# Hybrid decoder trunk: attention weights as differences of a scan, stick queries and keys projected as feature rows, narrower dilated scores

## Chip, core and metric

One core of a Trainium2 chip runs the whole program. TensorE multiplies and transposes, VectorE (DVE), ScalarE (ACT) and GpSimd (POOL) do elementwise work, and the queue of SyncE (SP) issues the transfers. The metric is the device time of one execution in microseconds.

## What is computed

Two layers, each `x = x + concat(A, B) @ w_out`, on x of 2048 x 1024 in fp32. One input projection of the normalised x gives queries, keys, values and gates for two mixers.

- A, stick-breaking attention, 4 heads of 64: `z = q k / 8`; `log_surv = log_sigmoid(z) - z` for earlier keys; `a = exp(log_sigmoid(z) + sum of log_surv over later keys)`; `o = a v`. So a weight is sigmoid(z) times the product of sigmoid(-z) over all keys between it and the query.
- B, dilated window attention, 12 heads of 64: three patterns (window 128 step 1, 512 step 4, 2048 step 16), each a softmax over at most 129 keys per query, mixed by their denominators. Queries and keys are normalised and partly rotated.

Each mixer's output is multiplied by a SiLU gate.

## The kernel before

Almost all products run in a rounded fp32 format (F32R); where precision asks for it, an operand is split into a high and a low part and three products are summed. The stages of a layer follow each other: normalise and transpose x (`prep` of `Project`), projection (`run`), stick attention (`_stick`), dilated attention (`_dilated`), output (`_output`). A planner orders the instructions of each engine, except that those marked `pin` keep their order in the program on TensorE.

**Projection.** `mm3` multiplies 128 tokens (stationary) by 512 columns of weights (streaming), in 8 steps of k with three products each. Two token blocks form a group; four PSUM banks (`pm`) hold two groups. First come the values of A (`narrow("sb", ...)`), then the list `wide`: queries and keys of A together (`"sb"`), three blocks of queries and keys of B (`"qk"`, evacuated by `qk_out`: squares, sum, power on GpSimd, multiply, rotation, split, transposes), a block of values of B. `tail` has the rest; gates go the other way round (weights stationary, 512 tokens streaming). Queries, keys and values of A are written to `sb_scr`, one row per token. During the last tail block, `inject` starts work of `_stick`.

**Stick.** `prep(pr, jq)` for a pair of heads and a quarter of the tokens loads rows of queries and keys, splits them into high and low parts, transposes 16 blocks (L504), copies them (L507) to feature rows, and lets two transfers swap the halves of the keys into `sh` (L509, L510). The first pair's four quarters are injected into the projection; the second pair's run between the first pair's units.
A unit is 128 queries against up to 512 keys, from late keys to early ones; a layer has 80 units of two heads. `front` makes the scores (L541, L542, and L544 for the mask), two sigmoids (L549, L550), a running product from the end (L551) and on GpSimd the weight (L557):

```
g = sigmoid(-z/8);  b = sigmoid(z/8)
r[k] = r[k+1] * g[k]          (scan, carried from unit to unit)
b = b * r[k+1]
```

`mid` transposes the weights (L570) and copies them (L572), the first head on ScalarE, the second on VectorE. `back` multiplies by the values (L584). `front` runs `LEAD` = 2 units ahead of `mid`; `back` is called for `BATCH` = 2 units at once. Slots: 6 for `r`, 6 for `g`, 6 for `b`, 6 for the copied weights.

**Dilated.** Six pairs of heads, three patterns, 16 blocks of 128 queries: 48 steps a pair. `front` makes four score products (two heads, two halves of the split, L732), adds the mask and takes the minimum on VectorE (L734), and exponentiates on ScalarE (L738). `mid` transposes (L753) and copies (L755), alternately on ScalarE and VectorE; `back` multiplies by values (L767) for four blocks. All score products stream 256 columns; pattern 0, and the first blocks of the other patterns, use only 128 of them. In later pairs, `stats_a` and `stats_b` work out the weights of the mixture of the pair before; `weigh` broadcasts them by a product (L837) and multiplies (L838), in steps 15 to 30, after `mid` and `back`. `mid` reads one of four `pe` slots.

The functions that the diff touches:

Of the kernel before, what the change touches and what calls it, by code (L numbers as in the profile page):

```python
# [115 lines left out]
def kernel(ctx, tc, x, norm_g, w_in, q_g, k_g, w_out, rope, masks, sel, out,  # L116
# [24 lines left out]
    for layer in range(depth):  # L141
        last = layer == depth - 1
        L = f"l{layer}"
        sb_scr = dram.tile([3, S, 256], F32, name=f"sb_{L}")
# [12 lines left out]
        sb = _stick(tc, mem, sb_scr, g_scr, mix, ident, ident_r)  # L157
# [5 lines left out]
        proj.run(sb_scr, v_scr, qk_scr, g_scr, inject)  # L163
# [25 lines left out]
class Project:  # L189
# [96 lines left out]
    def run(self, sb_scr, v_scr, qk_scr, g_scr, inject):  # L286
# [25 lines left out]

        def v_out(i, n, src, c):
# [10 lines left out]
        def sb_out(i, n, src, c):  # L324
            for j in range(n):
                nc.sync.dma_start(out=sb_scr[i + j].rearrange("(a c) d -> a c d", c=NT)[:, c],
                                  in_=src[:, 256 * j:256 * j + 256])
# [48 lines left out]
        wide = [("sb", 0, [(0, QA, 512)])]  # L376
# [28 lines left out]
        for bi, (kind, idx, parts) in enumerate(wide):  # L405
            nxt = wide[bi + 1][2] if bi + 1 < len(wide) else None
            for g in range(NT // 2):
# [5 lines left out]
                for k in range(NK) if edge else (None,):  # L413
                    for j in range(2):
                        for kk in range(NK) if k is None else (k,):
                            mm3(pss[j], 2 * g + j, kk, *self.wide(kk))
# [8 lines left out]
                if kind == "qk":  # L425
                    qk_out(idx, pss, 2 * g)
                    continue
                for j, ps in enumerate(pss):
                    st = stg.get([128, 512])
                    (nc.scalar.copy if j else nc.vector.tensor_copy)(st, ps)  # L430
                    (sb_out if kind == "sb" else v_out)(idx, 2, st, 2 * g + j)

        for bi, (kind, idx, parts) in enumerate(tail):
# [9 lines left out]
            for gi, (ct, tq) in enumerate(order):  # L443
# [4 lines left out]
                w = slice(128 * ct, 128 * ct + 128)  # L448
                ps = pm.get([128, 512])
                for k in range(NK):  # L450
                    nc.tensor.matmul(ps, wh[:, k, w], hT(tq, 0, k), start=k == 0, stop=False)  # L451
                    nc.tensor.matmul(ps, wh[:, k, w], hT(tq, 1, k), start=False, stop=False)  # L452
                    nc.tensor.matmul(ps, wl[:, k, w], hT(tq, 0, k), start=False, stop=k == NK - 1)  # L453
# [6 lines left out]
def _stick(tc, mem, sb_scr, g_scr, mix, ident, ident_r):  # L460
# [10 lines left out]
    raw_r = mem.ring("H0", "H1")  # L471
    q2_r = mem.ring("F12", "F13")
# [4 lines left out]
    r_s = Slices([wk0[:, i] for i in range(6)])  # L477
    gam = Slices([wk0[:, 6 + i] for i in range(6)])
    b_s = Slices([wk1[:, i] for i in range(6)])
    at_s = Slices([wk1[:, 6 + i] for i in range(6)])  # L480
    nc.gpsimd.memset(wk0[:, 6:12, 512:513], 1.0)
    qs_, ks1, ks2, vn, gt = {}, {}, {}, {}, {}

    def prep(pr, jq):
        cs = slice(128 * pr, 128 * pr + 128)
        rows = slice(512 * jq, 512 * jq + 512)
        raw = raw_r.get([128, 4, 2, 128])
        for s in range(2):
            nc.sync.dma_start(out=raw[:, :, s], in_=sb_scr[s, rows, cs].rearrange("(j p) d -> p j d", p=128))
        q2 = q2_r.get([128, 4, 4, 2, 64], F32R)  # L490
        rv = raw.rearrange("p j s (h d) -> p j (s h) d", d=64)
        nc.scalar.copy(q2[:, :, :, 0], rv)
        nc.vector.tensor_tensor(out=q2[:, :, :, 1], in0=rv, in1=q2[:, :, :, 0].bitcast(F32), op=ALU.subtract)
        sf = mem.get(setF[jq], [128, 4, 512], F32R)
        sh = mem.get(setH[jq], [128, 2, 512])
        for h in range(2):
            qs_[pr, jq, h] = sf[:, h]
            ks1[pr, jq, h] = sf[:, 2 + h]
            ks2[pr, jq, h] = sh[:, h].bitcast(F32R)
        for g in range(4):  # L500
            yield
            ps = t_r.get([128, 512], F32R)
            for j in range(4):
                nc.tensor.transpose(ps[:, 128 * j:128 * j + 128],  # L504
                                    q2[:, j, g].rearrange("p s d -> p (s d)"), ident_r)
            h = g % 2
            (nc.vector.tensor_copy if g % 2 else nc.scalar.copy)(sf[:, g], ps.bitcast(F32))  # L507
            if g == 3:
                nc.sync.dma_start(out=sh[0:64], in_=sf[64:128, 2:4].bitcast(F32))  # L509
                nc.sync.dma_start(out=sh[64:128], in_=sf[0:64, 2:4].bitcast(F32))  # L510

    def load(pr):
        cs = slice(128 * pr, 128 * pr + 128)
        vn[pr] = mem.get(("F5", "F6")[pr], [128, NT, 128])
        nc.sync.dma_start(out=vn[pr], in_=sb_scr[2, :, cs].rearrange("(j p) d -> p j d", p=128))
# [3 lines left out]
    yield lambda jq: [None for _ in prep(0, jq)], lambda: load(0)  # L519
# [12 lines left out]
    def front(u):  # L532
# [14 lines left out]
        for h, z in enumerate(zs):  # L547
            b, g, r = b_s.get(), gam.get(), r_s.get()
            nc.scalar.activation(g[:, 512 - n:512], z[:, :n], AF.Sigmoid, scale=-0.125)  # L549
            nc.scalar.activation(b[:, :n], z[:, :n], AF.Sigmoid, scale=0.125)  # L550
# [6 lines left out]
            nc.gpsimd.tensor_tensor(out=b[:, :n], in0=b[:, :n], in1=r[:, 1:n + 1], op=ALU.mult)  # L557
            prod[u].append(b)
        if pr == 0 and i % 4 == 0 and lo == 0:
            todo.append(prep(1, i // 4))  # L560
            next(todo[-1])

    def mid(u):
# [3 lines left out]
        for h, b in enumerate(prod.pop(u)):  # L567
# [4 lines left out]
            (nc.vector.tensor_copy if h else nc.scalar.copy)(at[:, :n], ps[:, :n])  # L572
# [21 lines left out]
    todo = []  # L594
    LEAD, BATCH = 2, 2
# [4 lines left out]
    for u in range(len(units)):  # L600
# [7 lines left out]
        for _ in range(max(1, len(todo))):  # L608
            while todo and next(todo[0], 0) == 0:
                todo.pop(0)  # L610
# [6 lines left out]
def _dilated(tc, mem, v_scr, qk_scr, g_scr, mix, masks, sel, ident, neg1):  # L617
# [9 lines left out]
    pe_s = Slices([pa[:, 0], pa[:, 1], pb[:, 0], pb[:, 1]])  # L627
    ta, tb = mem.get("H6", [128, 2, 2, 2, 128]), mem.get("H7", [128, 1024])
    td = mem.get("H5", [128, 2, 2, 2, 128])
# [75 lines left out]
    def front(g):  # L705
# [6 lines left out]
        u0 = 0  # L712
        if p == 0:
            w0 = min(b, 14) * 128
            u0 = 128 * b - w0
        else:
# [265 lines left out]
```

## Time and profile before

| | |
|---|---|
| median of 3 runs | 3229.11 us (3222.7 to 3229.73) |
| profiled execution | 3228.57 us, span 3226.8 us, mean granted clock 0.993 |
| busy in the span | TensorE 97%, VectorE 51%, ScalarE 48%, GpSimd 38% |
| first layer, about | normalising 125 us, projection 640, stick 251, dilated 396, output 198 |

The second layer repeats the first. A busy matmul row includes the drain of its result, so two rows that follow each other overlap; how fast matmuls follow is read from their starts.

### The profile page before, as it was taken

To read this page: it belongs to the slowest core of one execution; us is meant where nothing else is said; L and a number is where in the kernel's file an instruction comes from. 1 tells how busy PE (TensorE), PEld (TensorE's weight loads), DVE (VectorE), ACT (ScalarE), POOL (GpSimd) and SP (SyncE) were. 2 spreads that over 40 slices of the span, in tenths; PEclk is the share of its full clock that TensorE was granted. 3 is DMA by queue.
4 is the path that set the end of the run, shared out by engine and by line. 5 is a ranking of instruction groups with operands and counts; after the bars stand their busy time and mean duration, and the time that the engine had idled before them with its cause. 6 is when DMAs were issued, how large, how long until landed. Compare 5 with 4: busy or idle time off the path is not lost.

```text
span 3226.8 us, 59494 instructions
## 1 busy us (share of the span) xinstructions
PE 3137.9 (97%) x21968; PEld 2683.2 (83%) x21968; DVE 1648.3 (51%) x4147; ACT 1534.4 (48%) x4317; POOL 1234.4 (38%) x1302
## 2 busy tenths in 40 slices
PE   8999999999999999989999999999999999999899
PEld 8888888887777999878898888888877789988787
DVE  6134440015988777764141444301169887777721
ACT  5123331114878998962031233211158789988510
POOL 1067751102664444451010677511036734444500
PEclk9999999999999999999999999999999999999999
DMA  5123346317023556454442233463160235663443
GB/s 198 63 73 113 112 138 181 122 48 204 15 83 93 165 155 193 117 164 150 128 135 72 70 113 105 149 189 104 59 186 21 83 106 151 178 187 100 140 145 108
DMA packets 324066, 396.40 MB, mean 123 GB/s; under 512 B 20160, under 2 KB 270016, under 8 KB 313536
## 3 DMA queue, kind: packets, MB, share of 16 engines
q1 hardware_dynamic: 323776, 392.60, 40.0%
q8 instruction: 174, 2.85, 0.4%
q14 instruction: 116, 0.95, 0.1%
HBM read 235.24 MB, written 148.90 MB: 119 GB/s over the span
## 4 chain that ended last, share of the span: by engine, by line
PE 81%; DVE 5%; ACT 4%; POOL 4%; issue 3%; DMA 2%; SPq 0%; POOLq 0%; ACTq 0%; DVEq 0%
PE b L310 11%; PE b L311 11%; PE b L309 11%; PE b L732 7%; PE b L767 5%; PE b L753 5%; PE b L451 4%; PE b L453 4%; PE b L452 4%; PE b L935 4%; PE b L936 4%; PE b L932 3%; PE b L584 3%; PE b L367 2%; ACT H L738 2%
## 5 line engine op out<-in xcount | busy, mean ns | idle before, releaser
L738 ACT ACTIVATE H<-H,T 128x256 f32<-128x256 f32 (+1 forms) x1152 | 522.7, 457 | 45.9 <-DVE T L734 43.4
L311 PE MATMUL b<-F,F 128*128 128x512 f32 (+1 forms) x1344 | 484.1, 360 | 0.4 <-DVE F L282 0.3
L734 DVE CUSTOM_DVE_ANT_0 H<-b,M 128x256 f32<-128x256 f32 (+1 forms) x1152 | 368.6, 361 | 168.9 <-PE b L732 66.2
L732 PE MATMUL b<-F,F 128*128 128x256 f32 x2304 | 412.3, 303 | 0.3 <-DVE T L734 0.3
L557 POOL TENSOR_TENSOR G<-G,G 128x512 f32<-128x512 f32 (+3 forms) x320 | 320.5, 1017 | 228.5 <-DVE G L551 171.6
L551 DVE TENSOR_TENSOR_SCAN G<-G,b 128x513 f32<-128x513 f32 (+3 forms) x320 | 336.5, 1085 | 33.0 <-ACT G L550 32.7
L732 PEld LDWEIGHTS b<-F,F 128*128 128x128 f32 x2304 | 326.4, 190 | 20.1 <-issue 19.5
L310 PE MATMUL b<-F,G 128*128 128x512 f32 (+1 forms) x896 | 324.7, 362 | 0.0
L309 PE MATMUL b<-F,G 128*128 128x512 f32 (+1 forms) x896 | 324.3, 362 | 0.0
L310 PE MATMUL b<-F,F 128*128 128x512 f32 (+1 forms) x896 | 323.2, 361 | 0.0
L309 PE MATMUL b<-F,F 128*128 128x512 f32 (+1 forms) x896 | 321.9, 359 | 0.0
L753 PE MATMUL b<-ident,H 128*128 128x128 f32 x1800 | 292.9, 274 | 11.4 <-ACT H L755 5.5
L311 PEld LDWEIGHTS b<-F,F 128*128 128x128 f32 x1344 | 253.7, 189 | 38.4 <-DVE F L282 0.8
L135 POOL TENSOR_SCALAR U<-U 128x16 f32<-128x16 f32 (+1 forms) x80 | 33.7, 421 | 536.1 <-DVE U L334 315.5
L767 PE MATMUL b<-H,H 128*64 128x128 f32 x3600 | 229.8, 277 | 0.8 <-DVE H L755 0.8
L753 PEld LDWEIGHTS b<-ident,H 128*128 128x128 f32 x1800 | 215.6, 141 | 16.5 <-ACT H L755 8.6
L549 ACT ACTIVATE G<-b 128x512 f32<-128x512 f32 (+3 forms) x320 | 179.5, 563 | 103.6 <-PE b L542 87.8
L738 ACT ACTIVATION_READ_ACCUMULATOR H<-H,T 128x1 f32 x1152 | 219.3, 190 | 0.0
L767 PEld LDWEIGHTS b<-H,H 128*64 128x64 f32 x3600 | 193.8, 137 | 25.9 <-issue 23.4
L212 POOL TENSOR_TENSOR F<-H,F 128x1024 fp32r<-128x1024 f32 x22 | 53.9, 2456 | 380.7 <-ACT F L211 164.0
L333 ACT ACTIVATE H<-b 128x512 f32<-128x512 f32 x96 | 57.5, 600 | 294.8 <-PE b L311 293.8
L309 PEld LDWEIGHTS b<-F,G 128*128 128x128 f32 x896 | 168.9, 189 | 26.6
(165 smaller groups left out, 6844.2 us busy)
## 6 DMA issues: line engine op xcount, KB each, us to landing
qk_l<-H SPq DMA_DIRECT2D x192, 256.0 KB
F<-qk_l SPq DMA_DIRECT2D x48, 1024.0 KB
v_l<-S SPq DMA_DIRECT2D x288, 128.0 KB
H<-v_l SPq DMA_DIRECT2D x72, 512.0 KB
F<-qk_l SPq DMA_DIRECT2D x48, 512.0 KB
g_l<-S SPq DMA_DIRECT2D x64, 256.0 KB
G<-mixa_l SPq DMA_DIRECT2D x32, 448.0 KB
H<-in_w_in SPq DMA_DIRECT2D x24, 512.0 KB
```

Source lines behind the costliest of these rows:

```text
L309: nc.tensor.matmul(ps, hT(q, 0, k)[:, cs], wh, start=k == 0, stop=False)
L310: nc.tensor.matmul(ps, hT(q, 0, k)[:, cs], wl, start=False, stop=False)
L311: nc.tensor.matmul(ps, hT(q, 1, k)[:, cs], wh, start=False, stop=k == NK - 1)
L451: nc.tensor.matmul(ps, wh[:, k, w], hT(tq, 0, k), start=k == 0, stop=False)
L549: nc.scalar.activation(g[:, 512 - n:512], z[:, :n], AF.Sigmoid, scale=-0.125)
L551: nc.vector.tensor_tensor_scan(out=r[:, 0:n + 1][:, ::-1], data0=g[:, 512 - n:513][:, ::-1], data1=z[:, 0:1].to_broadcast([128, n + 1]), i ...
L557: nc.gpsimd.tensor_tensor(out=b[:, :n], in0=b[:, :n], in1=r[:, 1:n + 1], op=ALU.mult)
L732: pin(nc.tensor.matmul(sc[:, h], qb, kv, start=s == 0, stop=s == 1))
L734: nc.vector.tensor_tensor_reduce(out=pe[:, h, :un], in0=sc[:, h, u0:u0 + un], in1=mk[:, m0:m0 + un], scale=-0.125, scalar=3.0e38, op0=ALU. ...
L738: nc.scalar.activation(pe[:, h, :un], pe[:, h, :un], AF.Exp, scale=-1.0, bias=st[:, 0, p, h, b:b + 1], accum_out=st[:, 1, p, h, b:b + 1])
L753: pin(nc.tensor.transpose(tp[:, ch, h], pe[:, h, 128 * w:128 * w + 128], ident))
L767: pin(nc.tensor.matmul(ob[64 * h:64 * h + 64, b % 4], vq[(pr * 3 + p) * 2 + (b - ch) // 8][:, (b - ch) % 8, 64 * h:64 * h + 64], ts[:, ch, h],
```

## The change

The second sigmoid goes: since r[k] = r[k+1] g[k] and sigmoid(z) = 1 - sigmoid(-z), the weight is r[k+1] - r[k], a difference of the scan with itself. The slots for `r` and `g` become 4 each, those for the copied weights 10, `BATCH` becomes 4, and both copies of `mid` go to ScalarE. Queries and keys of the stick branch are projected with the weights stationary and the tokens streaming, split when they leave PSUM, and written as feature rows to `sq_scr`; `prep` only loads, and loads the keys a second time with halves exchanged. In the dilated stage score products have 128 columns where 128 are used, VectorE takes three of four copies, a fifth `pe` slot is made, and `weigh` and `gate` move from after `back` to between `front` and `mid`, two steps later.

```diff
-        sb_scr = dram.tile([3, S, 256], F32, name=f"sb_{L}")
+        sq_scr = dram.tile([2, 2, 2, 128, S], F32, name=f"sq_{L}")
+        sb_scr = dram.tile([S, 256], F32, name=f"sb_{L}")
...
+        def mmw(ps, ct, tq, k, wh, wl):
+            w = slice(128 * ct, 128 * ct + 128)
+            nc.tensor.matmul(ps, wh[:, w], hT(tq, 0, k), start=k == 0, stop=False)
+            nc.tensor.matmul(ps, wh[:, w], hT(tq, 1, k), start=False, stop=False)
+            nc.tensor.matmul(ps, wl[:, w], hT(tq, 0, k), start=False, stop=k == NK - 1)
...
+        def sq_out(ct, pss, tqs):
+            if tqs[0] == 0:
+                stq[ct] = [[mem.get(f"H{2 + 2 * l + u}", [128, 64, NT], F32R) for u in range(2)]
+                           for l in range(2)]
+            hi, lo = stq[ct]
+            for ps, tq in zip(pss, tqs):
+                pv = ps.rearrange("p (c a) -> p c a", c=4)
+                for u in range(2):
+                    hv, lv = (x[u].rearrange("p a c -> p c a")[:, 4 * tq:4 * tq + 4] for x in (hi, lo))
+                    src = pv[:, :, 64 * u:64 * u + 64]
+                    nc.scalar.copy(hv, src)
+                    nc.vector.tensor_tensor(out=lv, in0=src, in1=hv.bitcast(F32), op=ALU.subtract)
+            if tqs[1] == 3:
+                for u in range(2):
+                    for l, x in enumerate((hi, lo)):
+                        xu = x[u].rearrange("p a c -> p (a c)")
+                        for h in range(2):
+                            nc.sync.dma_start(
+                                out=sq_scr[ct // 2, ct % 2, h, 64 * l:64 * l + 64, 1024 * u:1024 * u + 1024],
+                                in_=xu.bitcast(F32)[64 * h:64 * h + 64])
...
-        wide = [("sb", 0, [(0, QA, 512)])]
+        wide = [("sq", 0, [(0, QA, 512)])]
...
-                            mm3(pss[j], 2 * g + j, kk, *self.wide(kk))
+                            if kind == "sq":
+                                mmw(pss[j], g // 2, 2 * (g % 2) + j, kk, *self.wide(kk))
+                            else:
+                                mm3(pss[j], 2 * g + j, kk, *self.wide(kk))
...
-    r_s = Slices([wk0[:, i] for i in range(6)])
-    gam = Slices([wk0[:, 6 + i] for i in range(6)])
+    r_s = Slices([wk0[:, i] for i in range(4)])
+    gam = Slices([wk0[:, 4 + i] for i in range(4)])
     b_s = Slices([wk1[:, i] for i in range(6)])
-    at_s = Slices([wk1[:, 6 + i] for i in range(6)])
+    at_s = Slices([wk1[:, 6 + i] for i in range(6)] + [wk0[:, 8 + i, :512] for i in range(4)])
...
+        sf = mem.get(setF[jq], [128, 4, 512])
+        sh = mem.get(setH[jq], [128, 2, 512])
         for s in range(2):
-            nc.sync.dma_start(out=raw[:, :, s], in_=sb_scr[s, rows, cs].rearrange("(j p) d -> p j d", p=128))
-        q2 = q2_r.get([128, 4, 4, 2, 64], F32R)
-        rv = raw.rearrange("p j s (h d) -> p j (s h) d", d=64)
-        nc.scalar.copy(q2[:, :, :, 0], rv)
-        nc.vector.tensor_tensor(out=q2[:, :, :, 1], in0=rv, in1=q2[:, :, :, 0].bitcast(F32), op=ALU.subtract)
+            nc.sync.dma_start(out=sf[:, 2 * s:2 * s + 2], in_=sq_scr[s, pr, :, :, ts].rearrange("h p t -> p h t"))
+        for l in range(2):
+            nc.sync.dma_start(out=sh[64 * l:64 * l + 64],
+                              in_=sq_scr[1, pr, :, 64 - 64 * l:128 - 64 * l, ts].rearrange("h p t -> p h t"))
...
-            nc.scalar.activation(b[:, :n], z[:, :n], AF.Sigmoid, scale=0.125)
...
-            nc.gpsimd.tensor_tensor(out=b[:, :n], in0=b[:, :n], in1=r[:, 1:n + 1], op=ALU.mult)
+            nc.gpsimd.tensor_tensor(out=b[:, :n], in0=r[:, 1:n + 1], in1=r[:, 0:n], op=ALU.subtract)
...
-            (nc.vector.tensor_copy if h else nc.scalar.copy)(at[:, :n], ps[:, :n])
+            nc.scalar.copy(at[:, :n], ps[:, :n])
...
-    LEAD, BATCH = 2, 2
+    LEAD, BATCH = 2, 4
...
-    pe_s = Slices([pa[:, 0], pa[:, 1], pb[:, 0], pb[:, 1]])
+    pe_s = Slices([pa[:, 0], pa[:, 1], pb[:, 0], pb[:, 1], tb[:, 512:1024].rearrange("p (h k) -> p h k", h=2)])
...
                 if p == 0:
-                    kv = kt[:, w0:w0 + 256]
+                    kv = kt[:, 128 * b:128 * b + 128]
                 else:
                     kv = kt.rearrange("p (c a) -> p c a", c=NT)[
-                        :, c::stp, w0:w0 + 2 * run].rearrange("p c (w a) -> p w c a", w=2)
-                pin(nc.tensor.matmul(sc[:, h], qb, kv, start=s == 0, stop=s == 1))
+                        :, c::stp, w0:w0 + run * un // 128].rearrange("p c (w a) -> p w c a", a=run)
+                pin(nc.tensor.matmul(sc[:, h, :un], qb, kv, start=s == 0, stop=s == 1))
...
-        (nc.vector.tensor_copy if g % 2 else nc.scalar.copy)(ts[:, :nch], tp[:, :nch])
+        (nc.scalar.copy if g % 4 == 1 else nc.vector.tensor_copy)(ts[:, :nch], tp[:, :nch])
...
             front(g + LEAD)
+        if pr and 17 <= t < 33:
+            weigh(pr - 1, t - 17)
+            if t % 4 == 0:
+                gate(pr - 1, (t - 17) // 4)
         mid(g)
...
-            elif 15 <= t < 31:
-                weigh(pr - 1, t - 15)
-                if t % 4 == 2:
-                    gate(pr - 1, (t - 15) // 4)
```

## Rows read from the trace of the kernel before

**Rows 1.** Windows, us: stick and dilated stages of the first layer, busy (and instructions) by engine

```profile
765.00:1015.80 250.80, 231.47 (x2114) 186.15 (x2112) 224.66 (x271) 184.80 (x416) 164.75 (x168) 0.98 0.28 80
1015.80:1412.00 396.20, 387.62 (x3983) 356.36 (x3982) 293.52 (x1388) 359.23 (x1366) 171.31 (x217) 1.00 0.55 158
```

**Rows 2.** Groups of instructions, stick stage, VectorE: busy us, mean ns, idle before

```profile
L551 DVE TENSOR_TENSOR_SCAN G<-G,b 128x513 f32<-128x513 f32 (+3 forms) x160 | 168.3, 1085 | 16.5 <-ACT G L550 16.5
L572 DVE COPY G<-b 128x512 f32<-128x512 f32 (+3 forms) x80 | 47.1, 590 | 4.0 <-PE b L570 3.8
L590 DVE TENSOR_TENSOR F<-b,F 128x512 f32<-128x512 f32 x7 | 7.9, 1134 | 0.0
L507 DVE CAST F<-b 128x512 fp32r<-128x512 f32 x10 | 6.8, 680 | 0.1
```

**Rows 3.** Groups, stick stage, ScalarE

```profile
L550 ACT ACTIVATE G<-b 128x512 f32<-128x512 f32 (+3 forms) x160 | 90.3, 567 | 0.0
L549 ACT ACTIVATE G<-b 128x512 f32<-128x512 f32 (+3 forms) x160 | 89.8, 563 | 52.1 <-PE b L542 44.1 <-PE b L544 7.9
L572 ACT COPY G<-b 128x512 f32<-128x512 f32 (+3 forms) x80 | 45.8, 573 | 3.2 <-PE b L570 3.1
```

**Rows 4.** Groups, stick stage, GpSimd

```profile
L557 POOL TENSOR_TENSOR G<-G,G 128x512 f32<-128x512 f32 (+3 forms) x160 | 160.2, 1017 | 114.3 <-DVE G L551 85.8 <-PE b L570 22.4 <-PE b L542 3.6
```

**Rows 5.** Timeline, TensorE, units in the stick stage: start us, us, count

```profile
788.23 0.50 PE L541 MATMUL b<-F,F 128*128 128x512 f32 x1
...
789.25 1.04 PE L570 MATMUL b<-ident,G 128*128 128x128 f32 x8
790.04 0.48 PE L541 MATMUL b<-F,F 128*128 128x512 f32 x1
...
792.12 1.97 PE L584 MATMUL b<-G,F 128*64 128x128 f32 x32
```

**Rows 6.** Groups, stick stage, TensorE

```profile
L542 PE MATMUL b<-H,F 128*128 128x512 f32 (+2 forms) x160 | 59.6, 372 | 5.8 <-DMA H<-F 5.8
...
L504 PE MATMUL b<-ident_r,F 128*128 128x128 f32 x72 | 9.4, 255 | 0.4 <-DVE F L507 0.3
L453 PE MATMUL b<-F,F 128*128 128x512 f32 x9 | 4.0, 444 | 0.0
```

**Rows 7.** Windows at the start of the stick stage (PEclk, DMA share, GB/s last)

```profile
760.00:765.00 5.00, 5.00 (x31) 4.23 (x31) 1.27 (x2) 1.24 (x2) 0.00 (x0) 1.00 1.16 290
770.00:775.00 5.00, 3.43 (x12) 3.07 (x13) 3.54 (x4) 3.71 (x8) 4.56 (x4) 0.56 0.85 213
```

**Rows 8.** Windows: pattern 0 of first pair; patterns 0, 1, 2 of third

```profile
1015.80:1032.00 16.20, 14.87 (x141) 13.16 (x139) 10.52 (x71) 15.12 (x70) 1.38 (x3) 1.00 0.71 203
1142.40:1162.20 19.80, 19.80 (x211) 17.61 (x209) 12.05 (x75) 17.77 (x76) 7.46 (x12) 1.00 1.06 264
1162.20:1186.70 24.50, 22.82 (x231) 21.22 (x230) 21.05 (x85) 21.36 (x79) 13.88 (x16) 1.00 0.44 137
1186.70:1210.30 23.60, 23.60 (x250) 22.19 (x249) 17.38 (x75) 22.15 (x79) 10.97 (x16) 1.00 0.44 130
```

**Rows 9.** Timeline, TensorE, transposes in the projection

```profile
300.62 1.47 PE L367 MATMUL b<-ident_r,H 128*128 128x128 f32 x16
```

**Rows 10.** Groups by shape, whole span, GpSimd

```profile
L138 POOL TENSOR_TENSOR U<-U,half 128x16 f32<-128x16 f32 x48 | 152.8, 3183 | 4.0
```

**Rows 11.** Timeline, TensorE, pattern 0 of the first pair

```profile
1024.43 0.28 PE L732 MATMUL b<-F,F 128*128 128x256 f32 x1
1024.55 0.38 PE L753 MATMUL b<-ident,H 128*128 128x128 f32 x2
```

**Rows 12.** Groups, whole span, all engines

```profile
L755 DVE COPY H<-b 128x512 f32<-128x512 f32 (+1 forms) x288 | 172.1, 597 | 1.7 <-PE b L753 1.5
...
L837 PE MATMUL b<-W,F 128*128 128x384 f32 x192 | 80.3, 418 | 10.3 <-POOL W L826 8.9 <-DVE G L838 1.1
...
L807 PE MATMUL b<-S,M 128*32 128x128 f32 x96 | 14.5, 273 | 0.0
```

## What I expect, before the result

> **What bounds the kernel now.** I first read the windows by stage [rows 1], because the share of busy time over the whole span mixes five stages with different limits. TensorE is busy in all of them, but its matmul rows include a drain that overlaps the next matmul, so "busy" there is not "full". In the stick stage (250.8 us a layer) VectorE is busy for 224.7 us while TensorE is at 231.5; in the dilated stage (396.2 us) TensorE shows 387.6, ScalarE 359.2, VectorE 293.5.
>
> Second, the groups of the stick stage. VectorE carries the 160 scans (168.3 us), half of the copies of the transposed weights (47.1), and the casts of the old preparation [rows 2]. ScalarE does two sigmoids a scan (90.3 + 89.8) and the other half of the copies [rows 3]; GpSimd one product a scan, 160.2 us [rows 4]. The reader should see that no engine but VectorE is both near the length of the stage and made of work that queues behind itself.
>
> Third, what TensorE really needs there, from starts and not from durations [rows 5]: a full unit's four score products go from 788.23 to 789.25, 1.02 us; its eight transposes to 790.04, 0.79 us or 0.099 each; 32 output matmuls (two units) take 1.97 with the last drain, 0.06 each. A layer has, by the code, 80 units, 56 of them full. 544 transposes make 54 us, 1088 output matmuls 65, the scores 56 x 1.02 = 57 and about 19 for the 24 shorter units (0.8 each, an estimate), and 25 matmuls of the gate projection that run inside the window (9 on the line of [rows 6]) about 6 at the scores' 0.255: 201 us. With the 72 transposes of the preparation [rows 6] at 0.085, 207. So TensorE waits for some 44 of 250.8 us, although it looks 92% busy: this stage belongs to VectorE. A little of it is start-up: score products wait 5.8 us for the swapped keys' transfer [rows 6], and after it the granted clock is 0.56 of full, near the lower of the two levels, for 770 to 775 us, while the transfers run at 213 to 290 GB/s [rows 7].
>
> Fourth, the dilated stage by pattern [rows 8]. Pattern 0 in a later pair takes 19.8 us for 16 blocks with TensorE busy throughout, ScalarE 17.8, VectorE 12.1. In the first pair it takes 16.2 with ScalarE at 15.1: there ScalarE is nearly as short. Pattern 1 in a later pair, where the weighting runs, takes 24.5 with VectorE already at 21.1. Pattern 2 fills TensorE (23.6 of 23.6), with ScalarE at 22.2.
>
> **Part 1: scan differences.** One sigmoid of two goes: 160 ScalarE instructions a layer, 90.3 us [rows 3]. ScalarE was not the bound, so this is worth only what is put in its place: all copies move to ScalarE, 80 more at 0.573, 46 us. ScalarE goes from 184.8 to about 140 (and loses the casts of the preparation). VectorE loses 47.1 of copies and 6.8 of casts [rows 2], and some subtractions beside them, down to 171 or less. GpSimd keeps 160 instructions; a subtraction of two shifted slices of one tile for a product of two tiles, taken at the same 1017 ns (bounds: nothing saved, or, if two reads of one tile cost as the slowest full one, 10% more, still under 180).
>
> So the order of needs a layer becomes TensorE 201, VectorE 171, GpSimd 165, ScalarE 140, and TensorE is late next. It will not run without waits, because output matmuls now come four units at a time. Such a batch is 3.8 us in which no scores are made, and only two units are scored ahead. After it TensorE asks for four units in 4 x 1.81 = 7.2 us, while four units are eight scans, 8.7 us at the mean [rows 2]. The cycle is 11.0 us if the two units ahead cover the difference, and 12.5 if each batch waits 1.5 us for the last scan and its subtraction. I take 0.9 us a batch (between, as 8.7 - 7.2 has to come from the 3.8), 20 batches: 18 us. Start-up and the change of pair keep 4 us. 201 + 18 + 4 = 223 us, a gain of **28 us a layer**; bounds 205 (no waits) and 239 (1.5 us a batch and the old start-up), 46 and 12 us.
>
> **Part 2: queries and keys as feature rows.** The projection has the same 384 products of 512 columns, and weights and activations change sides. The 128 transposes a layer go. 72 lie in the stick stage (counted above); 56 lie before it, among projection matmuls, where TensorE is full: 56 x 0.085 = **4.8 us a layer**. The price 0.085 is from 16 such transposes in 1.47 us [rows 9], 0.092 each with the last one's drain, a little less without it. The swap through a transfer is replaced by loading rows twice; per preparation four loads of 1.5 MB in all stand for two loads and two swaps of 1.0 MB. They are issued before the values and gates of the pair, so the third and fourth units no longer stand behind the casts, copies and swaps.
>
> The new evacuation is 32 ScalarE and 32 VectorE instructions of 256 elements with a stride of 16 on the output. Bounds: 0.35 us if the stride is free, 0.57 at the rate of the strided gate product, 1.13 for 512 [rows 2]. Either way a pair of banks is empty within 3 us, against 11 us or more of matmuls of the next pair (48 at 0.23 to 0.255): nothing, hidden by the projection. What may show: each quarter writes 2 MB through four pages that the next quarter, and then the first normalised block of the dilated queries, must reuse. At 264 to 290 GB/s [rows 7, 8] and behind 2 MB of weights, that is 8 to 15 us after the last copy. The first block's chain then starts up to 9 us late. This chain holds its banks through a 3.18 us power on GpSimd [rows 10] and several passes before it, and has some 3 us to spare. I take **2 us a layer lost**, bounds 0 and 6.
>
> **Part 3: 128 columns where 256 were computed.** 84 score products a pair, 1008 in all, shrink. A 256-column product is followed by the next instruction after 0.12 us (1024.43 to 1024.55, [rows 11]). No 128-column product of this kind is in the trace. The nearest is the transpose in the same number format with a weight load of its own, 0.085. Below it lies half of 0.12, 0.06. Above it lies a plain fp32 product, which goes as two instructions (96 on the line for 48 products, [rows 12]), 0.2 us. I take 0.085: 0.035 x 1008 = 35 us of TensorE time.
>
> By the row of transposes, then, four products of a block shrink by 0.14 us. The Trainium skill (TensorE: Matmul & The Clock Gate, LDWEIGHTS) speaks against it: a weight load costs its columns over 1.2 GHz, 107 ns for 128, whatever is streamed. By that rule 1008 products would give back 13 us and not 35. The trace does not agree for the transposes, which each load 128 columns and follow each other within 0.092.
>
> Where does it land? In pattern 0 of the ten later pairs TensorE is the bound and ScalarE has 2 us of room, which the moved copies raise to 3: 64 x 0.035 = 2.2, I take 2.0 each, 20 us. In the two first pairs ScalarE holds it to 0.5 each. Pattern 1 of a later pair gains nothing: copies go from half to three quarters on VectorE, 4 x 0.6 [rows 12], which makes 21.1 into 23.5 of about 24. Pattern 1 of the first pairs and pattern 2: 3 us in all.
>
> **Part 4: weighting behind the scores, a fifth buffer.** The broadcast waits 8.9 us in all for the weights from GpSimd [rows 12]. It moves two blocks later, 2.5 us more than the 0.9 of each wait, so I count 7. The buffer takes VectorE waits away where VectorE is not late: nothing. Against it, 5 us for VectorE at its limit in pattern 1. Sum of the dilated stage: 20 + 1 + 3 + 7 - 5 = **26 us in both layers**, bounds 0 and 50.
>
> **Sum.** 2 x 28 + 2 x 4.8 - 2 x 2 + 26 = 87.6. The profiled execution took 3228.57 us, 0.5 under the median of the runs. 3228.6 - 87.6 = **3141 us**. Its own range is 3115 to 3170.
>
> **Rivals.**
> *Starved batches.* The batch of four waits its full 1.5 us and the start-up stays as it is; 239 us a stage, so 32 us less gained: 3173 us. For it: 8.7 against 7.2. Against it: 3.8 us of batch in which the scans go on.
> *VectorE takes over the dilated stage.* Moved copies make weighting blocks longer by what pattern 0 gains, and the projection stall is 6: 3141 + 26 + 8 = 3175 us. For it: 23.5 of 24 us; against it: pattern 0 and 2 leave VectorE a third idle.
> *Everything lands.* No batch waits, 0.06 a product: about 3105 us.
> *The weight load sets the step.* Then a narrower stream changes nothing: the step stays at the 0.12 of [rows 11], and part 3 gives back none of its 24 us: 3165 us. For it: every product has its own load of 128 columns. Against it: the transposes of [rows 9] have one too. This is the rule of the page named above; with its own 107 ns it would be 3156 us.
> *Slower: short products go in two passes.* If a product under 256 columns in this format costs as the plain fp32 one, 0.2 or more (0.218 as two transposes of [rows 5] with their waits), 1008 products add 0.1 each, 100 us, where TensorE is already the bound, in place of the gain: 3141 + 26 + 100 = 3267 us. It decides from about 0.18 us a product. For it: before, nothing narrower than 256 columns is computed in this format, and narrower needs are padded. Against it: transposes of 128 columns in this format are quick.
>
> **Chances.** Forecast 0.50, starved batches 0.14, VectorE 0.11, the weight load 0.10, everything lands 0.07, two passes 0.08. The range from 3105 to 3190 leaves out the two passes and the edges. A difference under 0.2% (6.5 us) is about what this kernel's runs can't tell from none. Faster 0.89, same 0.03, slower 0.08.
>
> **What would show it.** Stick stage near 223 us with VectorE at about 171 and TensorE's own waits on the scan's subtraction once a batch; no rows for the second sigmoid, the transposes of the preparation and the swap; score products of pattern 0 stepping at 0.085 us instead of 0.12; pattern 0 of a later pair near 17.8 us; weighting blocks of pattern 1 at VectorE's limit; the first square after the quarters late by no more than a few us. The forecast is wrong if the 128-column product steps at 0.12 or more, if the stick stage stays above 235, or if the first dilated block stalls the projection by more than 10 us.

## The result, and the profile after

The changed kernel takes 3175.53 us (median of 4 runs, 3174.8 to 3177.16) against 3226.94 for the kernel before (median of 4, 3222.7 to 3229.73): a ratio of 0.9842, 95% interval 0.9825 to 0.986. That is 51 us gained; 88 were forecast. The direction holds, and so does the range from 3105 to 3190 us; the forecast's own range, 3115 to 3170, does not, and its point is 34 us too low.

The profiled execution took 3175.44 us, its span 3173.7. Windows of the first layer after the change: the projection behind the first preparation, the stick stage, the dilated stage. The columns are those of [rows 1].

```profile
125.50:760.40 634.90, 634.90 (x3203) 534.85 (x3202) 181.43 (x257) 145.06 (x244) 235.74 (x205) 1.00 0.38 119
760.40:994.00 233.60, 219.13 (x2042) 178.43 (x2040) 173.85 (x177) 147.87 (x323) 148.45 (x168) 0.98 0.34 103
994.00:1386.20 392.20, 385.74 (x3983) 348.54 (x3982) 324.53 (x1461) 337.40 (x1298) 170.33 (x217) 1.00 0.55 158
```

Against [rows 1]: the stick stage starts 4.6 us earlier (760.4 for 765.0; forecast were 4.8 less 2 of stall) and lasts 233.6 us instead of 250.8 (223 forecast); the dilated stage lasts 392.2 instead of 396.2 (13 us a layer forecast). 4.6 + 17.2 + 4.0 is 25.8 us a layer, 51.6 for two, of 53.1 between the spans.

Groups of the stick stage after: VectorE's scan, ScalarE's one sigmoid and the copies, GpSimd's subtraction and two casts, TensorE's transposes.

```profile
L565 DVE TENSOR_TENSOR_SCAN G<-G,b 128x513 f32<-128x513 f32 (+3 forms) x160 | 162.2, 1078 | 42.4 <-ACT G L564 33.8 <-POOL G L571 7.9 <-issue 0.3
```

```profile
L564 ACT ACTIVATE G<-b 128x512 f32<-128x512 f32 (+3 forms) x160 | 82.0, 559 | 65.9 <-PE b L557 52.4 <-PE b L559 12.5
L585 ACT COPY G<-b 128x512 f32<-128x512 f32 (+3 forms) x160 | 79.5, 548 | 18.4 <-PE b L583 17.3
```

```profile
L571 POOL TENSOR_TENSOR G<-G 128x512 f32<-128x512 f32 (+3 forms) x160 | 144.0, 913 | 94.6 <-DVE G L565 81.7 <-PE b L559 2.6 <-PE b L583 1.6
L704 POOL CAST F<-S 128x512 fp32r<-128x512 f32 x4 | 2.4, 612 | 11.9 <-DMA S<-in_sel 11.9
L681 POOL CAST F<-F 128x512 fp32r<-128x512 f32 x4 | 2.3, 615 | 3.1 <-DMA F<-qk_l 3.1
```

```profile
L583 PE MATMUL b<-ident,G 128*128 128x128 f32 x544 | 80.6, 281 | 8.9 <-POOL G L571 8.3
```

Three things are to be seen. What Part 1 takes away is gone: one sigmoid group instead of the two of [rows 3], VectorE's copies of [rows 2] on ScalarE. VectorE fell from 224.7 to 173.9 us (171 forecast), and its scans wait 42 us, 34 of them for the sigmoid: it is no longer the bound. The subtraction takes 913 ns where the product of [rows 4] took 1017. And GpSimd stands idle 11.9 and 3.1 us in front of eight casts, for transfers; these casts don't belong to this stage. They round data of the dilated stage, which starts at 994.

The timelines show what that costs, first on GpSimd, then on TensorE.

```profile
787.43 3.36 POOL L571 TENSOR_TENSOR G<-G 128x512 f32<-128x512 f32 x4 [2.56 <-PE b L559]
798.34 0.61 POOL L704 CAST F<-S 128x512 fp32r<-128x512 f32 x1 [7.55 <-DMA S<-in_sel]
798.91 1.04 POOL L571 TENSOR_TENSOR G<-G 128x512 f32<-128x512 f32 x1
```

```profile
795.89 0.40 PE L557 MATMUL b<-H,F 128*128 128x512 f32 x1
800.00 1.11 PE L583 MATMUL b<-ident,G 128*128 128x128 f32 x4 [3.72 <-POOL G L571]
```

```profile
901.13 0.39 PE L557 MATMUL b<-H,F 128*128 128x512 f32 x1
903.83 1.48 PE L583 MATMUL b<-ident,G 128*128 128x128 f32 x5 [2.31 <-POOL G L571]
```

The cast of 798.34 has waited 7.55 us for the transfer of `in_sel`, and the next subtraction, whose scan was ready, stands behind it in GpSimd's queue. TensorE starts nothing between 795.89 and 800.00; the same happens at 901.13 with the casts of L681. In a window that takes in the end of the first hole, and in one right behind the second, the granted clock (third number from the end) is near the lower level:

```profile
798.00:805.00 7.00, 4.55 (x21) 3.97 (x22) 3.41 (x4) 1.91 (x5) 6.66 (x8) 0.52 0.11 40
904.00:907.00 3.00, 2.92 (x11) 2.25 (x11) 2.26 (x2) 1.34 (x3) 3.00 (x5) 0.51 0.02 5
```

The holes cost 3.9 + 2.4 us beyond an ordinary step, and the clock at most 7 x 0.48 + 3 x 0.49 = 4.8: up to 11 us a layer. In the kernel before the same casts stood in the same stage, but all of them between 899 and 919 us, and waited 1.2 and 0.8 us:

```profile
L695 POOL CAST F<-S 128x512 fp32r<-128x512 f32 x4 | 2.4, 610 | 1.2 <-DMA S<-in_sel 1.1
L672 POOL CAST F<-F 128x512 fp32r<-128x512 f32 x4 | 2.3, 614 | 0.8 <-DMA F<-qk_l 0.8
```

In the dilated stage the windows of [rows 8] are now, for the first pair's pattern 0 and for patterns 0, 1 and 2 of the third pair:

```profile
994.00:1008.70 14.70, 14.23 (x140) 12.78 (x138) 11.84 (x75) 13.20 (x64) 1.37 (x3) 1.00 0.74 216
1118.60:1138.30 19.70, 19.16 (x210) 16.77 (x208) 13.23 (x79) 16.84 (x73) 8.46 (x13) 1.00 1.07 257
1138.30:1161.10 22.80, 22.79 (x229) 20.34 (x227) 21.09 (x88) 19.16 (x74) 12.03 (x14) 1.00 0.48 147
1161.10:1185.10 24.00, 24.00 (x253) 22.41 (x251) 21.05 (x84) 21.10 (x76) 11.79 (x17) 1.00 0.44 136
```

Pattern 0 of the third pair, for which 17.8 was forecast, takes 19.7 (19.8 before) and is still TensorE's. VectorE in pattern 1 is at 21.1 of 22.8, not at its limit; two weighted blocks went over to pattern 2, which is 0.4 longer.

### The profile page after: what moved, and what is told of

It reads as the page before. It is cut to its first block, busy times and chain, and to the rows that moved or that the text cites. A ratio compares the mean times of both kernels' runs of the same rounds, so it can differ in the third digit from the quotient of the medians.

```text
span 3173.7 us, 58878 instructions
## 1 busy us (share of the span) xinstructions
PE 3100.5 (98%) x21712; PEld 2643.9 (83%) x21712; DVE 1618.6 (51%) x4131; ACT 1425.4 (45%) x4013; POOL 1201.7 (38%) x1302
## 4 chain that ended last, share of the span: by engine, by line
PE 87%; DVE 4%; POOL 2%; issue 2%; ACT 2%; DMA 2%; SPq 0%; DVEq 0%; POOLq 0%; ACTq 0%
PE b L311 9%; PE b L310 9%; PE b L312 9%; PE b L737 8%; PE b L772 6%; PE b L758 6%; PE b L316 6%; PE b L318 6%; PE b L317 6%; PE b L940 4%; PE b L941 4%; PE b L937 4%; PE b L597 4%; PE b L583 2%; PE b L395 2%
## 5 line engine op out<-in xcount | busy, mean ns | idle before, releaser
L737 PE MATMUL b<-F,F 128*128 128x256 f32 (+1 forms) x2304 | 408.2, 301 | 2.8 <-DVE T L739 2.8
L312 PE MATMUL b<-F,F 128*128 128x512 f32 (+1 forms) x1152 | 409.2, 355 | 0.4 <-DVE F L283 0.3
L565 DVE TENSOR_TENSOR_SCAN G<-G,b 128x513 f32<-128x513 f32 (+3 forms) x320 | 324.6, 1079 | 84.8 <-ACT G L564 69.0
L571 POOL TENSOR_TENSOR G<-G 128x512 f32<-128x512 f32 (+3 forms) x320 | 287.9, 913 | 190.8 <-DVE G L565 154.7
L737 PEld LDWEIGHTS b<-F,F 128*128 128x128 f32 x2304 | 312.1, 191 | 31.7 <-issue 26.3
L311 PE MATMUL b<-F,G 128*128 128x512 f32 (+1 forms) x768 | 274.6, 358 | 0.0
L310 PE MATMUL b<-F,G 128*128 128x512 f32 (+1 forms) x768 | 274.2, 357 | 0.0
L311 PE MATMUL b<-F,F 128*128 128x512 f32 (+1 forms) x768 | 273.4, 356 | 0.0
L310 PE MATMUL b<-F,F 128*128 128x512 f32 (+1 forms) x768 | 272.1, 354 | 0.0
L312 PEld LDWEIGHTS b<-F,F 128*128 128x128 f32 x1152 | 217.6, 189 | 30.8 <-DVE F L283 0.8
L760 DVE COPY H<-b 128x512 f32<-128x512 f32 (+1 forms) x432 | 241.5, 559 | 1.2 <-PE b L758 0.9
L317 PE MATMUL b<-F,F 128*128 128x512 f32 x576 | 224.5, 390 | 0.0
L564 ACT ACTIVATE G<-b 128x512 f32<-128x512 f32 (+3 forms) x320 | 164.0, 558 | 133.0 <-PE b L557 105.8
L487 DVE TENSOR_TENSOR S<-b,S 128x512 f32<-128x512 f32 x64 | 44.3, 692 | 318.8 <-ACT S L486 318.8
```

The lines of the kernel that those rows point to most:

```text
L310: nc.tensor.matmul(ps, hT(q, 0, k)[:, cs], wh, start=k == 0, stop=False)
L311: nc.tensor.matmul(ps, hT(q, 0, k)[:, cs], wl, start=False, stop=False)
L312: nc.tensor.matmul(ps, hT(q, 1, k)[:, cs], wh, start=False, stop=k == NK - 1)
L317: nc.tensor.matmul(ps, wh[:, w], hT(tq, 1, k), start=False, stop=False)
L565: nc.vector.tensor_tensor_scan(out=r[:, 0:n + 1][:, ::-1], data0=g[:, 512 - n:513][:, ::-1], data1=z[:, 0:1].to_broadcast([128, n + 1]), i ...
L571: nc.gpsimd.tensor_tensor(out=b[:, :n], in0=r[:, 1:n + 1], in1=r[:, 0:n], op=ALU.subtract)
```

## The experiments

All are edits of the changed kernel; the gains named in us are against its 3175.53. Ratios are to the kernel before, with their 95% intervals. e1 to e4 ran on one chip, e5 to e8 on a second, e9 and e10 on a third; the medians of before on the three are 3227.39, 3225.94 and 3227.04.

**e1: casts of the dilated stage behind the last subtraction** (by `pin`, here for GpSimd's queue).

```
-                    eng.tensor_copy(
+                    (pin if pr == 0 else lambda x: x)(eng.tensor_copy(
...
-        nc.gpsimd.tensor_copy(selr[:, 4 * i:4 * i + 4], t)
+        pin(nc.gpsimd.tensor_copy(selr[:, 4 * i:4 * i + 4], t))
```

> Four casts of the selection matrix and the first pair's eight casts of queries for pattern 2, which belong to the dilated stage, are held in GpSimd's queue behind the last subtraction of the stick stage. Nothing is left out. Theory 'GpSimd's queue': in the changed kernel these casts were put among the subtractions and waited 7.6 and 3.1 us for transfers, so the two long holes of TensorE (4.1 and 2.7 us, each followed by a stretch at the lower clock) go: about 10 us a layer, 20 us in all, about 3156 us, stick stage 223 us. Rival 'starved batches': the holes come from four units of output matmuls in one go, the casts only fill the time: 3175 us within 4.

Measured 3156.99 us (3156.02 to 3158.53), ratio 0.9785 (0.977 to 0.9799): 18.5 gained. The windows of its stick stage, and of the stretch where the first hole was:

```profile
760.20:983.30 223.10, 215.09 (x2042) 175.53 (x2040) 173.26 (x177) 147.24 (x323) 145.26 (x162) 1.00 0.35 104
```

```profile
798.00:805.00 7.00, 6.99 (x80) 5.73 (x78) 6.22 (x7) 4.56 (x11) 5.97 (x8) 1.00 0.29 77
```

The stage is 10.5 us shorter, 80 matmuls start in a stretch where 21 did, and the clock stays at the upper level; the casts now start at 980.54 us and later. So the two queue holes, with the clock that fell at them, are the difference between the forecast 223 us and 233.6.

**e2: output matmuls of two units at a time.**

```
-    LEAD, BATCH = 2, 4
+    LEAD, BATCH = 2, 2
```

> Output matmuls come two units at a time instead of four; nothing else. Theory 'GpSimd's queue': between the holes TensorE has no gap over 0.6 us, so the size of the batch is worth little: 3175 us within 8. Rival 'starved batches' (1.5 us a batch waited, 20 batches a layer): the waits go, 20 to 30 us a layer at most and 10 at least, so 3155 us or lower.

Measured 3155.46 us (3151.14 to 3156.63), ratio 0.9777 (0.9763 to 0.9792): 20 gained, as much as by e1, so the batch is not the small matter that I expected. Its stick stage is 221.3 us long:

```profile
796.00:799.00 3.00, 0.24 (x2) 0.00 (x0) 0.06 (x1) 0.90 (x2) 2.14 (x3) 1.00 0.08 24
799.00:802.00 3.00, 2.42 (x18) 1.86 (x18) 2.76 (x3) 1.58 (x5) 3.00 (x4) 1.00 0.27 87
```

In the first layer the first hole, with the casts, is still there, 3.3 us (TensorE starts at 795.85 and then at 799.15), but the clock does not fall behind it, and the one at 897 has shrunk to 1.5 us. In the second layer the first hole is 3.6 us long (2366.18 to 2369.77), and there the clock does fall:

```profile
2371.40:2374.80 3.40, 3.40 (x21) 2.87 (x21) 1.65 (x3) 2.12 (x5) 3.40 (x5) 0.50 0.24 71
```

**e3: 256 columns for the dilated scores again**, everything else as changed.

```
...
-                    kv = kt[:, 128 * b:128 * b + 128]
+                    kv = kt[:, w0:w0 + 256]
...
-                pin(nc.tensor.matmul(sc[:, h, :un], qb, kv, start=s == 0, stop=s == 1))
+                pin(nc.tensor.matmul(sc[:, h], qb, kv, start=s == 0, stop=s == 1))
...
```

> Score products of the dilated stage stream 256 columns again in all blocks, as before the change; the rest of the change stays. Theory 'the weight load sets the step' (0.113 us at 128 columns, 0.12 at 256): 1008 products get 0.007 us each, 7 us, so 3182 us within 4. Rival, the prediction's price (0.085): 20 us or more, 3196 us.

Measured 3184.41 us (3182.5 to 3188.11), ratio 0.9871 (0.9856 to 0.9886): 8.9 lost. 1008 products are worth 8.9 us, 9 ns each, and not the 35 ns of the forecast.

**e4: the whole dilated stage as before** (the function `_dilated` of the kernel before in the changed kernel).

> The whole dilated stage as before the change (256 columns, copies alternating, four buffers, weighting after the outputs); projection and stick stage as after. If stick and projection bring 43 us of the 51 and the dilated stage 8 to 10, as the stage windows say: 3184 us. If the prediction's 26 us were there and lost elsewhere: 3200 us.

Measured 3184.74 us (3182.67 to 3188.05), ratio 0.9873 (0.9856 to 0.9889): 9.2 lost. All of the changed dilated stage is worth what its 128 columns are worth; the moved weighting, the fifth buffer and the moved copies come to nothing together.

**e5: e1 and e2 together.**

> Casts of the dilated stage behind the stick stage in GpSimd's queue, and output matmuls two units at a time. With the two at once: the stick stage of the batch-of-two kernel (221 us) still has holes of TensorE of 3.3, 1.5 and twice 0.6 us at the casts; without them 216 us, 10 us less in both layers, 3145 us. If the two edits cure the same waits: 3153 to 3157 us.

Measured 3141.93 us (3141.57 to 3146.27), ratio 0.974 (0.9727 to 0.9754): 33.6 gained. The window of its stick stage:

```profile
759.80:975.40 215.60, 212.01 (x2041) 176.30 (x2039) 174.32 (x177) 144.56 (x323) 145.26 (x162) 1.00 0.35 107
```

Without the holes the batch of two shortens the stage by 223.1 - 215.6 = 7.5 us a layer, 15 in two, and the medians of e1 and e5 differ by 15.1. So batch and queue are two costs. The gains of e1 and e2 alone add up to 38.6, 5 more than e5 gives: this fits that both take away a part of the same loss, the holes and the low clock at them, but was not taken apart further.

**e6: copies of the dilated weights alternate between the engines as before.**

```
-        (nc.scalar.copy if g % 4 == 1 else nc.vector.tensor_copy)(ts[:, :nch], tp[:, :nch])
+        (nc.vector.tensor_copy if g % 2 else nc.scalar.copy)(ts[:, :nch], tp[:, :nch])
```

> The copies of the dilated stage alternate again between ScalarE and VectorE; the rest of the change stays. Pattern 2 of the later pairs takes 24.0 us in the changed kernel and 23.5 before it; if the copies that VectorE took are the cause, it goes back, 20 x 0.5... ten later pairs by 0.45: 5 us faster, 3171 us, unless ScalarE then slows pattern 0 by as much. Rival, the copies moved to VectorE relieve ScalarE in pattern 0: 3180 us.

Measured 3177.82 us (3176.69 to 3178.75), ratio 0.9848 (0.9835 to 0.9862): 2 us above the changed kernel and inside what can be told from none. The 5 us that I charged for these copies are not there.

**e7: weighting and gate two blocks earlier, where they were.**

```
-        if pr and 17 <= t < 33:
-            weigh(pr - 1, t - 17)
...
+            elif 15 <= t < 31:
+                weigh(pr - 1, t - 15)
...
```

> Weighting and gating back to their old place, after the outputs and two steps earlier; the rest of the change stays. Prediction's count for the move: 7 us, so 3182 us; pattern 1 of the later pairs is 0.9 us shorter in the changed kernel than before, times ten: 3184 us. If the move is worth nothing: 3175 us within 3.

Measured 3173.65 us (3172.32 to 3175.18), ratio 0.9836 (0.9822 to 0.9849). The row of [rows 12] for the broadcast is back in part, beside that of the changed kernel:

```profile
L842 PE MATMUL b<-W,F 128*128 128x384 f32 x192 | 79.8, 415 | 5.4 <-POOL W L831 3.7 <-DVE G L843 1.5
```

```profile
L842 PE MATMUL b<-W,F 128*128 128x384 f32 x192 | 68.2, 355 | 5.6 <-DVE G L843 5.4
```

The move takes away TensorE's wait for GpSimd (3.7 us), but TensorE then waits for VectorE instead (5.4): 5.4 us idle against 5.6. The wait was renamed, not removed; the 7 us of credit are not there.

**e8: e5 with the alternating copies of e6.**

> Casts behind the stick stage, batches of two, alternating copies in the dilated stage: 5 us under the kernel with the first two, 3140 us, if the copies cost what pattern 2 shows; the same within 3 if not.

Measured 3149.85 us (3143.55 to 3150.81), ratio 0.9755 (0.9742 to 0.9768): 8 us more than e5 at the medians, on the same chip. TensorE's transposes in the first layer's dilated stage wait longer for the copies, first e8, then e5:

```profile
L758 PE MATMUL b<-ident,H 128*128 128x128 f32 x884 | 148.1, 278 | 9.2 <-DVE H L760 6.2 <-ACT H L760 2.8
```

```profile
L758 PE MATMUL b<-ident,H 128*128 128x128 f32 x887 | 147.4, 277 | 2.0 <-DVE H L760 1.0 <-ACT H L760 0.6
```

One such wait of 1.3 us at 982 is followed by a granted clock of 0.66 from 980 to 990 us, where e5 has 1.00. e6 has waits like these and lost nothing by them on balance, so why they cost 8 us here and 2 there is shown only as far as this stretch of clock.

**e9: the second product of each score in pattern 0 streams 64 columns and not 128** (half of its columns left out; the weight load stays).

```
+                if p == 0 and s:
+                    pin(nc.tensor.matmul(sc[:, h, :64], qb, kv[:, :64], start=False, stop=True))
+                    continue
```

> In pattern 0 the second product of each pair of score products streams 64 of its 128 columns, so half of the low parts' share of the scores is left out. Theory 'the weight load sets the step': the step from the full product to the half one and from the half one to the next stay at about 0.11 us, since each loads 128 columns of weights. Rival 'the stream sets it': a product of 64 columns is followed by the next within 0.07 to 0.09 us.

A single execution, 3186.06 us. Its total is not used: TensorE has holes of 1.4 to 1.6 us in later pairs, with the lower clock behind five of them, that have nothing to do with the question. What counts is the time from block to block in pattern 0 of the first pair: four products and two transposes. Before, then the changed kernel, then e9:

```profile
1024.69 0.72 PE L732 MATMUL b<-F,F 128*128 128x256 f32 x4
1025.24 0.38 PE L753 MATMUL b<-ident,H 128*128 128x128 f32 x2
1025.38 0.73 PE L732 MATMUL b<-F,F 128*128 128x256 f32 x4
```

```profile
1001.72 0.64 PE L737 MATMUL b<-F,F 128*128 128x128 f32 x4
1002.20 0.41 PE L758 MATMUL b<-ident,H 128*128 128x128 f32 x2
1002.36 0.64 PE L737 MATMUL b<-F,F 128*128 128x128 f32 x4
```

```profile
1002.71 0.31 PE L740 MATMUL b<-F,F 128*128 128x128 f32 x1
1002.85 0.25 PE L738 MATMUL b<-F,F 128*128 128x64 f32 x1
1002.93 0.31 PE L740 MATMUL b<-F,F 128*128 128x128 f32 x1
...
1003.15 0.44 PE L761 MATMUL b<-ident,H 128*128 128x128 f32 x2
1003.35 0.31 PE L740 MATMUL b<-F,F 128*128 128x128 f32 x1
```

From block to block: 0.69 us at 256 columns, 0.64 at 128, and 0.64 with half of every second product left out. Within a block of e9 a full and a half product together take 0.22 us (1002.71 to 1002.93), 0.11 each. The single steps are not 0.11 each, as I had expected, but 0.14 and 0.08. The 0.08 behind a half product is what the rival foretold, so by the steps alone neither expectation holds. The block decides more: four products take 0.44 us to the first transpose (1002.71 to 1003.15) where they took 0.48 (1001.72 to 1002.20), and the two transposes take that time back. Per block a stream below 128 columns gives nothing, and from 256 to 128 it gives 0.05 us in four products. So the stream is not what limits a block at 128 columns. That the weight load is, is argued and not shown: no run changes the load alone.

**e10: e5 with the weighting where it was (e7's edit).**

> Casts behind the stick stage, batches of two, weighting and gating at their old place. If the old place is as good as the new one: 3140 to 3144 us. If the later place hides the wait for the weights now that the rest is shorter: 7 us more than with the two edits alone, 3149 us.

Measured 3137.24 us (3133.47 to 3139.22), ratio 0.9723 (0.9709 to 0.9736): 38 under the changed kernel, 90 under the kernel before, and the fastest version. Its median is 4.7 us under that of e5, on another chip and with overlapping intervals, and with a mean granted clock of 0.995 to 0.997 in its executions against 0.993 to 0.995, so that this step alone is not certain.

## Why the prediction was right, and where its sizes were off

**What bounds the stick stage: as forecast, by the rows.** With the copies gone VectorE fell to 173.9 us (171 forecast) and now waits, while TensorE is late next. No run gives VectorE its copies back, or brings back the second sigmoid, by itself; that VectorE was the bound is argued from these rows. The 17.2 us of the stage also hold 72 transposes less (6.1 us by the prediction's price) and the transfers named under part 2.

**Part 1, the waits: the mechanism was right, one term was missing, and the rest agrees in part by luck.** The forecast was 201 of work, 18 of batch waits and 4 of start-up. The 223.1 us of e1 equal that sum. That a batch of four costs something is shown by e5, 7.5 us a layer more than a batch of two. But the parts are others. TensorE is idle for 8.0 us of e1's stage (223.10 - 215.09), and its wait for the subtraction, which was to come once a batch, is 1.8 us in all:

```profile
L583 PE MATMUL b<-ident,G 128*128 128x128 f32 x544 | 78.2, 275 | 2.4 <-POOL G L571 1.8
```

Late starts that hide behind the drain of the matmul before are not in these figures. Counted from the starts in the trace, an estimate, the steps that come over 0.12 us later than usual for their kind add up to some 16 us in e1 and 5 in e5. So waits and start-up are some 16 us and not 22, and the work is some 207 and not 201: scores 80 (76 in the working), transposes 58 (54), output matmuls 63 (65), gates 6 (6). The two errors cancel.

What the working had not got is the 10.5 us of e1. I had counted GpSimd's busy time alone; the eight casts of the dilated stage, which stand in its queue in both kernels, were no term of the sum. In the kernel before they waited 2.0 us in all; in the changed kernel the first of them stands at 774 us, and they waited 15.0. So this loss came with the new order of the queue, and did not lie hidden behind VectorE before. Why the planner put the casts there was not looked into. *Starved batches* got 0.14 and gave 239 us and 3173 in all: its numbers came close, while its mechanism is a part of what happened.

**Part 1, GpSimd's price: off to the good side.** 913 ns and not 1017, 16 us a layer of GpSimd. It lies beside other work.

**Part 2: right.** The stage starts 4.6 us earlier, with the stall in it: 5.0 for the 4.8 of the transposes, less 0.4 for the 2 of the stall. The first matmul of the gates, behind all queries, keys and values, starts at 590.54, in the kernel before at 590.15.

```profile
590.42 0.28 PE L312 MATMUL b<-F,F 128*128 128x256 f32 x1
590.54 0.40 PE L316 MATMUL b<-G,F 128*128 128x512 f32 x1
```

The prediction put the 5.8 us for the swapped keys [rows 6] down to start-up. They are two waits, and the longer one stands where the second pair's keys come in:

```profile
771.57 0.76 PE L542 MATMUL b<-H,F 128*128 128x512 f32 x1 [2.17 <-DMA H<-F]
903.61 0.64 PE L542 MATMUL b<-H,F 128*128 128x512 f32 x1 [3.60 <-DMA H<-F]
```

In the changed kernel the same products wait for no transfer:

```profile
L557 PE MATMUL b<-H,F 128*128 128x512 f32 (+2 forms) x160 | 59.1, 370 | 0.0
```

So part 2 took two holes out of the stick stage before the casts put two others in. Each pair of holes had its stretches of low clock: 0.50 from 771.6 to 777.4 us and 0.53 from 903.6 to 907.2 in the kernel before.

**Part 3: the step that failed.** It was "I take 0.085", the step of the transposes of [rows 9], for the 128-column product. In the changed kernel the steps are 0.11, and 0.14 behind the first product of a block: 0.48 us for four products, 0.12 each in the mean, the mark at which the prediction called itself wrong. What is gained is 9 ns a product by e3 and 13 from block to block. The rival *the weight load sets the step*, to which I gave 0.10, had the size nearly right. I had dismissed it because the transposes have a load of 128 columns too. But the rows of weight loads, which I had not read, tell the two apart. In pattern 0 of the first pair before:

```profile
L732 PEld LDWEIGHTS b<-F,F 128*128 128x128 f32 x65 | 8.6, 189 | 1.0 <-issue 0.7 <-PE b L732 0.3
L753 PEld LDWEIGHTS b<-ident,H 128*128 128x128 f32 x26 | 3.2, 140 | 1.7 <-ACT H L755 1.6
```

and for the transposes of [rows 9]:

```profile
L367 PEld LDWEIGHTS b<-ident_r,H 128*128 128x128 f32 x16 | 1.5, 140 | 0.1
```

The row of a product's load is 189 ns long, that of a transpose's 140 in both places. Steps of 0.085 with loads of 140 and of 0.11 with loads of 189 go together; the trace of before would have told that the transpose is not the right row. That the load makes the step is not shown by this. The Trainium skill (TensorE: Matmul & The Clock Gate, LDWEIGHTS) gives the time of a load as its columns over 1.2 GHz, 107 ns for 128, whatever is streamed. As an estimate from it, the six loads of a block, four products and two transposes, are 0.64 us, and both the changed kernel and e9 take that; the transposes of [rows 9], within 0.092 of each other, do not agree with it.

So Part 3 was sized at 24 us over both layers and is worth 9.

**Part 4: a credit and a debit that are not there.** The 7 and the 5 us are both about nothing (e7, e6). In the credit I took a wait's end for a gain without asking what TensorE waits for next: it is VectorE's multiplication (L843).

**The sum.** Forecast 87.6. By the windows of two layers the stick stage gives 34.4 instead of 56, its earlier start 9.2 instead of 9.6 - 4, and the dilated stage 8 instead of 26: 51.6. The 36 missing are 21.6 + 18 - 3.6. Of the first, e1 gives back 18.5 by the order of one queue; of the second, 15 were not to be had from narrower products.

**The slower rival** (two passes, 0.2 us a product) did not occur: products of 128 columns, and of 64, go in one instruction each (2304 rows for the 576 blocks of four, 384 for e9's).

## What to carry to other kernels

When the engine that was late is relieved, read the queue of the engine that comes next for instructions of a later stage, and where the new order has put them: here casts that waited for a transfer held up the subtractions behind them. Take the price of a new matmul from a row of the same kind, its weight load included, and not only of the same width. A narrower stream helps only while the stream is the limit; here halving 256 columns gave some 10 ns a product, and half of 128 nothing in the block. Where a wait is to be removed, name what ends last after it, before it is credited.

## What the runs showed of the hardware that was not expected

- The granted clock did not follow the length of TensorE's hole. It fell at holes of 4.1 and 2.7 us (changed kernel), at one of 1.3 us (e8) and at one of 3.6 us (e2, second layer), and stayed at the upper level at one of 3.3 us (e2, first layer). What decides stays open.
- On GpSimd a subtraction of two shifted slices of one tile takes 913 ns in the mean, a product of two tiles 1017, over the same 160 shapes. Of the full shapes, 128x512, every subtraction takes 1.04 us, while the products take 1.09 at the median and about 1.3 in the slowest quarter. Whether operation, operands or the busier VectorE of the kernel before makes the difference was not tried.
- The step of one product depends on its neighbour: a 128-column and a 64-column product with a load each take 0.14 and 0.08 us, 0.22 together (e9).
